# One more PSUM bank for the transposing and gelu tiles, other gather rates, and another DRAM layout of the gate matrix in a one-layer hybrid encoder kernel

## The chip, the cores and the metric

The kernel runs on one core of one Trainium2 chip. The metric is the device time of one execution in microseconds (us). One launch computes the whole layer.

## What is computed

The reference is one layer over 16 learned meta tokens and 1024 tokens of width 1024, in float32:

```
n  = rmsnorm(h)
h += W_out( sig(g_a) * W_oa(MLA(n)) + sig(g_b) * W_ob(GLA(n)) )
h += PEER(rmsnorm(h))
```

MLA is chunk-causal attention with 8 heads, GLA a gated linear attention with 4 heads. PEER is a mixture of 16384 one-row experts: for each token, 8 heads choose 16 experts each, by the two best-16 lists of 128 sub-keys; the output is

```
out[t] = sum over the 128 chosen e of  gate[t,e] * gelu(u[e] . n2[t]) * v[e]
```

The change lies in the PEER part and in the buffers of the mixing part.

## The kernel before, in words

**Stages.** Tokens come in two groups of 512. MLA of group 0, mix and route of group 0, MLA of group 1, mix of group 1 (`mix`, about 1290 to 1680 us), route of group 1 (`route`, about 1690 to 1950 us), then `dense` until the end. Each float32 product is three matmuls (`mm3`) on a high and a low part of each operand: `split` (lines 78 to 82) casts the high part on ScalarE (L79) and subtracts the low part on VectorE (L80).

**Two ways to do the experts.** Tokens 0 to 447 are done by gather (tokens 384 to 447 split differently from the rest): `gather_all` fetches rows of u and v by index, 128 rows of 4 KB each time, with an indirect DMA issued by GpSimd (L115), and VectorE does the dot (L1361) or the add into the output (L1377) for each. There are 832 such steps in all, on 6 row buffers (`NROW`). The generator is drawn forward by `bg`: each call of `weights` (one 512 KB weight tile) draws `self.rate` steps. The rates are the `R_` constants: 2.4 in the building of the gate matrix, 2.5 (`R_VONLY`) while only V stages run, 3.3 (`R_DENSE`) after that. A gather waits for the high cast of the weight tile that came before it in the program (`self.pace`).

**The dense way.** The other 640 tokens (five blocks of 128, `DB`) are multiplied with all experts, 128 groups of 128 experts. `u_stage` makes the gelu of one group (48 matmuls in two halves, each half in one PSUM bank of tag `tr`, read by the gelu on ScalarE, L1466). `v_stage(q, half)` takes four groups (`EG`), scales their activations by the gates (`coef`, L1504 copies the last 64 columns on ScalarE, L1505 multiplies the others on VectorE), splits them, and accumulates in five banks of tag `mm`, which VectorE adds into `acc` (L1530). The u stages of the first 58 groups (`NLEAD`) are done ahead and their activations kept in DRAM (`d_act`). From V stage 25 on, two u stages stand between two V stages.

**The gate matrix.** `gate_matrix` builds gate[expert, token] from one-hot products, 32 tokens at a time, in a stage tile of 16 KB per partition, and stores it to DRAM in `d_gate` (L1628): 20 stores of 2 MB. In the same stretch (1950 to about 2325 us) 31 lead u stages run. In `dense`, `gates(q, k, 4)` loads a quarter of one four-group's gates (L1492): 128 loads of 320 KB.

**Order.** Loads and stores of the program are issued by the SP queue in order. Within each engine the order of instructions is set at build time by a planner that simulates the program with its own costs, earlier lines of the program first; a wait at the head of an engine holds all that stands behind it. Weight tiles are loaded one ahead: raw tile, high and low part have two buffers each.

**PSUM.** There are 8 banks. In the mixing and the dense part, tag `tr` has 2 and tag `mm` 5.

Of the kernel before, what the change touches and what calls it, by code (L numbers as in the profile page):

```python
# [17 lines left out]
PSUM = bass.MemoryType.PSUM  # L18
DRAM = bass.MemoryType.DRAM

P = 128
# [7 lines left out]
NC = D // P  # L29
# [3 lines left out]
NK = 128  # L33
# [7 lines left out]
ND = len(DB) * P  # L41
# [4 lines left out]
EG = 4  # L46
# [11 lines left out]
BANKS = [dict(zip(("S", "tr", "mm", "pv"), map(int, str(x)))) for x in (BA, BB)]  # L58
NGA, NGR, F_MLA = 14, 14, 0.9
RA0, NRU, NLATE = 7, 22, 5  # L60
R_MLA, R_MIX, R_ROUTE, R_BUILD, R_VONLY, R_DENSE = 0.0, 2.8, 0.7, 2.4, 2.5, 3.3


class Layer:
# [94 lines left out]
    def build(self, debug=None):  # L159
# [12 lines left out]
        with ExitStack() as ctx:  # L172
            tc, nc, a = self.tc, self.nc, self.a
# [11 lines left out]
            dt = lambda n, s: dram.tile(s, F32, name=n)  # L185
# [14 lines left out]
            self.d_act = dt("d_act", [NLEAD, P, NU])  # L200
            self.d_n2t = dt("d_n2t", [2, P, NC, NU - GT])
            self.d_wl = dt("d_wl", [NKEPT, P, D])
            self.d_gate = dt("d_gate", [P, ND // 32, NK * 32])
            self.small = self.pool(ctx, "small", 3)
            self.sm = self.small
            with ExitStack() as c0:
# [11 lines left out]
                first = self.pool(early, "ck1", side="right")  # L218
# [299 lines left out]
    def mla_heads(self, ctx):  # L518
# [16 lines left out]
        for u in range(HA * 2):  # L535
# [9 lines left out]
            if gi == 0:  # L545
                self.merge(vals, fill)
                if h + 1 < HA:
                    self.load_wkv(h + 1)
                    self.head_tiles(h + 1)
                if u % 4 == 0 and h + 2 < HA:  # L550
                    if u == 0:
                        self.load_wq(1)
                    self.pair_tiles(h // 2 + 1)
                for f in late_fns:
                    f()
                    self.bg(self.rate)
                    self.beside(F_MLA)
            else:
                mix = []
                for i in range(max(len(fill), len(late_fns))):  # L560
                    mix += fill[i:i + 1] + late_fns[i:i + 1]
                self.merge(vals, mix)
# [238 lines left out]
    def mix_pools(self, ctx):  # L801
        if self.grp == 0:
            self.g1 = self.pool(ctx, "yA")
        self.psum = self.pool(ctx, "gpsum", 2, space=PSUM)
        self.wk = self.pool(ctx, "gw", 2)
        if self.grp == 0:
            self.arp = self.pool(ctx, "arpA", 2)
        if self.grp == 0:
            self.wp = self.wk
        self.nj = "gt"  # L810
        with self.tc.high_priority(offset=400):
            self.ya = self.load_ya(self.grp)
# [131 lines left out]
    def mix(self, g):  # L944
        nc = self.nc
        st = [{} for _ in range(4)]
        if g:
            self.warm(WARM[1], "mm", 5)
        first = self.gla_proj(g, 0, st[0], ("w_oa", 0))
        next(first)  # L950
        self.gla_logs(g)
        self.run(first)
        inner = self.gla_inner(g, 0, st[0])
        self.weave(self.branch_a(g, *self.ya), inner, 0.8)
        self.yb = self.t(self.g1, [P, NC, GT], F32R, "yh"), self.t(self.g1, [P, NC, GT], F32R, "yl")
        first = (NGA, NGR)[g]
        for h in range(1, 4):
            nxt = ("w_gq", h + 1) if h < 3 else (self.gate_keys() + [("w_ob", 0)])[first]
            self.weave(self.gla_proj(g, h, st[h], nxt), inner, 1.8)
            self.run(inner)  # L960
            inner = self.gla_inner(g, h, st[h])
        self.weave(self.raw_gates(g, range(first, 2 * NC), ("w_ob", 0), "tr", 2), inner, 1.0)
        self.run(inner)
        if g == 0 and NGF:
            self.fetch_n(self.nh, self.nl)
        self.run(self.branch_b(g))
# [499 lines left out]
            self.nc.scalar.activation(at[:, ts], ps[:, :HD], AF.Gelu)  # L1466

    def lead_gate(self, key, nxt):
        self.run(self.raw_gate(1, self.gate_keys().index(key), nxt, "tr", 2))

    def lead_u(self, key, nxt):
        e = key[1]
# [6 lines left out]
    def dense(self, ctx):  # L1479

        nc, a = self.nc, self.a
        self.psum = self.pool(ctx, "dpsum", 2, space=PSUM)
        self.wk = self.pool(ctx, "dw", 2)
        ng = NK // EG
        ndb = len(DB)
# [2 lines left out]
        def gates(q, k, n):  # L1488
            if q >= ng:
                return  # L1490
            bs = slice(k * ND // 32 // n, (k + 1) * ND // 32 // n)
            nc.sync.dma_start(gbuf[:, q % 2, bs].rearrange("p b e t -> p b (e t)"), self.d_gate[:, bs, q * EG * 32:(q + 1) * EG * 32])  # L1492

        def load_act(e):
            if e < NLEAD:
# [3 lines left out]
        def coef(q, j):  # L1499
            cf = coefs[q, j] = self.t(self.wk, [P, 2, ND], F32R, "cf", NCF)  # L1500
            at = acts.pop(q * EG + j)
            at3 = at.rearrange("p (b t) -> p b t", t=32)
            m = NU // 32
            nc.scalar.copy(at3[:, m:], gbuf[:, q % 2, m:, j])  # L1504
            nc.vector.tensor_tensor(at3[:, :m], at3[:, :m], gbuf[:, q % 2, :m, j], ALU.mult)  # L1505
            self.split(cf[:, 0], cf[:, 1], at)

        def v_stage(q, half):
            ps = [self.t(self.psum, [P, 512], F32, "mm", 5) for _ in range(ndb)]
            for i in range(EG // 2):  # L1510
                key = ("vb", q * EG // 2 + i, half)
                wh, wl = self.weights(key, order.get(key))
                gates(q + 2, 2 * half + i, 4)
                if q == 0 and half == 0:
                    for k in (2 * i, 2 * i + 1):
                        gates(1, k, 4)
                if q == 0 and i == EG // 2 - 1:
                    cs = slice(half * 512, (half + 1) * 512)
                    for k, b in enumerate(DB):
                        nc.sync.dma_start(acc[:, k, cs], self.d_h[b * P:(b + 1) * P, cs])  # L1520
                for j in range(2):
                    e = 2 * i + j
                    cf = coefs[q, e]
                    s = slice(j * 512, (j + 1) * 512)
                    for b in range(ndb):
                        ts = slice(b * P, (b + 1) * P)
                        self.mm3(ps[b], cf[:, 0, ts], cf[:, 1, ts], wh[:, s], wl[:, s], e == 0, e == EG - 1)
            for b in range(ndb):
                o = acc[:, b, half * 512:(half + 1) * 512]
                nc.vector.tensor_tensor(o, ps[b], o, ALU.add)  # L1530
# [29 lines left out]
        gbuf = self.t(self.wk, [P, 2, ND // 32, EG, 32], F32, "big")  # L1560
        for k in range(4):
            gates(0, k, 4)
# [11 lines left out]
        for x in seq[nlead:]:  # L1574
            if x[0] == "v":
                q, half = x[1:]
# [15 lines left out]
    def gate_matrix(self):  # L1592

        nc = self.nc
        G8 = 8
        iota = self.iota[:, None, :].broadcast_to([P, G8, NK])
        for d, blk in enumerate(DB):
            pk = self.picks[blk]  # L1600
            while blk == HB and not self.half_done:
                next(self.G)
            stage = self.t(self.wk, [P, NK, 32], F32, "big")
            pt = self.t(self.psum, [P, 4, P], F32, "tr")
            for i in range(2):
                nc.tensor.transpose(pt[:, i], pk["ij"][:, i].rearrange("p h k -> p (h k)"), self.ident)
            nc.tensor.transpose(pt[:, 2], pk["gate"].rearrange("p h k -> p (h k)"), self.ident)
            tt = self.t(self.wk, [P, ND], F32, "at", NAT)[:, 0:3 * P].rearrange("p (a t) -> p a t", a=3)
            nc.scalar.copy(tt, pt[:, 0:3])
            yield  # L1610
            for t32 in range(4):
                if t32:
                    stage = self.t(self.wk, [P, NK, 32], F32, "big")
                for q in range(4):
                    oh, gh = [self.t(self.wk, [P, 2 * ND], F32, "cf", NCF)[:, 0:NK * G8].rearrange("p (t j) -> p t j", j=NK) for _ in range(2)]
                    t = t32 * 32 + q * G8
                    tb = lambda i: tt[:, i, t:t + G8, None].broadcast_to([P, G8, NK])
                    for k in range(G8):
                        nc.vector.tensor_scalar(gh[:, k], self.iota, tt[:, 1, t + k:t + k + 1], tt[:, 2, t + k:t + k + 1], ALU.is_equal, ALU.mult)  # L1619
                    nc.vector.tensor_tensor(oh, iota, tb(0), ALU.is_equal)  # L1620
                    for k4 in range(2):
                        ps = self.t(self.psum, [P, 4, NK], F32, "mm", 5)
                        for k in range(4):
                            kk = k4 * 4 + k
                            self.gm_last = nc.tensor.matmul(ps[:, k], oh[:, kk], gh[:, kk], start=True, stop=True)  # L1625
                        nc.scalar.copy(stage[:, :, q * G8 + k4 * 4:q * G8 + k4 * 4 + 4], ps.rearrange("p k j -> p j k"))
                        yield
                nc.sync.dma_start(self.d_gate[:, d * 4 + t32], stage.rearrange("p j t -> p (j t)"))  # L1628


def host(inputs):
# [71 lines left out]
```

## Time and profile before

| | |
|---|---|
| median of 3 runs | 3832.95 us (3827.49 to 3835.6) |
| the profiled execution's own time | 3828.28 us |
| its span, first to last instruction | 3826.5 us |
| TensorE (PE) busy | 3551.3 us, 93% |
| VectorE (DVE) busy | 2999.0 us, 78% |
| ScalarE (ACT) busy | 1320.1 us, 34% |
| GpSimd (POOL) busy | 1523.7 us, 40% |
| mean granted TensorE clock | 0.968 |

PE leads in the whole, but the shares differ from stage to stage: from 1950 us on, DVE is busy for nearly as long as PE. Matmuls are pipelined, so a busy PE is not PE at its peak.

### The profile page before, as it was taken

The page shows a single profiled execution, that of the slowest core. Times are in us where ns is not written, and L with a number is a line of the kernel's source. Part 1 is how long each engine was busy: PE and PEld are TensorE (multiplying, and loading weights), DVE is VectorE, ACT ScalarE, POOL GpSimd, SP SyncE. Part 2 cuts the span into 40 slices and gives each one's busy share as a digit, 9 for nine tenths or more (in the row PEclk, how much of TensorE's full clock was granted, in tenths as well). Part 3 has the DMA queues.
Part 4 walks back from the last instruction along what each step waited for, and adds up shares of the span by engine and source line. Part 5 has one row for each costly group of instructions (what it writes and reads, how often), then busy time and mean ns, then how long its engine had stood idle before and what let it go on. Part 6 is the DMA issues. An engine that isn't in the chain of part 4 may idle for free.

```text
span 3826.5 us, 56688 instructions
## 1 busy us (share of the span) xinstructions
PE 3551.3 (93%) x20380; PEld 3088.1 (81%) x20385; DVE 2999.0 (78%) x6559; ACT 1320.1 (34%) x2851; POOL 1523.7 (40%) x1199
## 2 busy tenths in 40 slices
PE   8899998999799999899999998999999999999996
PEld 8787797777688788679898997777788888888885
DVE  5545444379877667559999997999988988898898
ACT  4656333232366334222244333222222222222221
POOL 2432333334332344322232223444455555555555
PEclk9999999999899999899999999999999999999998
DMA  4544634665324998665567879999999889999888
GB/s 160 173 159 141 222 131 130 192 212 186 124 69 114 341 353 299 268 225 203 171 227 275 288 280 372 332 342 344 332 334 338 303 315 325 322 348 322 298 324 318
DMA packets 390779, 976.98 MB, mean 255 GB/s; under 512 B 40464, under 2 KB 155664, under 8 KB 387680
## 3 DMA queue, kind: packets, MB, share of 16 engines
q1 hardware_dynamic: 242048, 508.50, 37.8%
q0 software_dynamic: 148448, 464.86, 34.6%
q8 instruction: 160, 2.62, 0.3%
q14 instruction: 123, 1.01, 0.1%
HBM read 825.61 MB, written 147.51 MB: 254 GB/s over the span
## 4 chain that ended last, share of the span: by engine, by line
PE 31%; DVE 24%; DMA 9%; issue 5%; ACT 1%; SPq 0%; POOL 0%; ACTq 0%; DVEq 0%; POOLq 0%
PE mm L86 6%; PE mm L87 6%; PE mm L88 6%; DVE cf L1619 4%; DVE acc L1377 3%; DVE row L1361 3%; DVE wl L80 3%; PE tr L88 3%; PE tr L86 3%; DMA wr<-in_uT 3%; PE tr L87 3%; DVE cf L1620 2%; DVE big L1530 2%; DMA row<-in_u,ids 2%; DMA row<-in_v,ids 1%
## 5 line engine op out<-in xcount | busy, mean ns | idle before, releaser
L115 POOL DMA_INDIRECT row<-in_v,ids x384 | 494.6, 1288 | 692.3 <-DVE acc L1377 274.1
L115 POOL DMA_INDIRECT row<-in_u,ids x384 | 479.5, 1249 | 590.8 <-issue 129.9
L86 PE MATMUL tr<-ar,wh 128*128 128x288 f32 x2048 | 616.9, 302 | 32.0 <-ACT at L1466 32.0
L79 ACT CAST wh<-wr 128x1024 fp32r<-128x1024 f32 x344 | 360.4, 1048 | 747.9 <-PE mm L88 302.8
L87 PE MATMUL tr<-ar,wh 128*128 128x288 f32 x2048 | 610.8, 299 | 0.0
L88 PE MATMUL tr<-ar,wl 128*128 128x288 f32 x2048 | 602.7, 301 | 8.5 <-DVE wl L80 8.1
L1361 DVE CUSTOM_DVE_ANT_0 row<-row,n2b 128x1024 f32<-128x1024 f32 x448 | 544.1, 1221 | 60.8 <-DMA row<-in_u,ids 51.0
L87 PE MATMUL mm<-wl,cf 128*128 128x512 f32 x1280 | 508.9, 398 | 5.1 <-DVE wl L80 5.0
L1377 DVE SCALAR_TENSOR_TENSOR acc<-row,act,acc 128x1024 f32<-128x1024 f32 x384 | 491.9, 1281 | 22.2 <-DMA row<-in_v,ids 20.0
L88 PE MATMUL mm<-wh,cf 128*128 128x512 f32 x1280 | 507.8, 397 | 0.0
L86 PE MATMUL mm<-wh,cf 128*128 128x512 f32 x1280 | 443.8, 398 | 15.0 <-DVE big L1530 8.6
L86 PEld LDWEIGHTS tr<-ar,wh 128*128 128x128 f32 x2048 | 392.4, 192 | 38.8 <-ACT at L1466 36.6
L80 DVE TENSOR_TENSOR wl<-wr,wh 128x1024 fp32r<-128x1024 f32 x264 | 324.6, 1229 | 103.2 <-ACT wh L79 98.9
L88 PEld LDWEIGHTS tr<-ar,wl 128*128 128x128 f32 x2048 | 387.5, 191 | 11.7 <-DVE wl L80 11.7
L87 PEld LDWEIGHTS tr<-ar,wh 128*128 128x128 f32 x2048 | 392.3, 192 | 2.1
L80 POOL TENSOR_TENSOR wl<-wr,wh 128x1024 fp32r<-128x1024 f32 x80 | 194.4, 2433 | 326.2 <-ACT wh L79 307.2
L86 PEld LDWEIGHTS mm<-wh,cf 128*128 128x128 f32 x1280 | 238.1, 188 | 80.5 <-ACT wh L79 9.9
L87 PEld LDWEIGHTS mm<-wl,cf 128*128 128x128 f32 x1280 | 241.9, 189 | 65.7 <-DVE wl L80 8.2
L88 PEld LDWEIGHTS mm<-wh,cf 128*128 128x128 f32 x1280 | 242.0, 189 | 58.8
L1530 DVE TENSOR_TENSOR big<-mm,big 128x512 f32<-128x512 f32 x320 | 204.4, 680 | 19.0 <-PE mm L88 18.9
L1466 ACT ACTIVATE at<-tr 128x288 f32<-128x288 f32 x212 | 87.0, 410 | 345.9 <-PE tr L88 326.1
L1625 PE MATMUL mm<-cf,cf 128*128 128x128 f32 x1280 | 158.4, 277 | 28.5 <-DVE cf L1620 28.5
(448 smaller groups left out, 7747.6 us busy)
## 6 DMA issues: line engine op xcount, KB each, us to landing
wr<-in_uT SPq DMA_DIRECT2D x128, 512.0 KB
wr<-in_vb SPq DMA_DIRECT2D x128, 512.0 KB
d_gate<-big SPq DMA_DIRECT2D x20, 2048.0 KB
big<-d_gate SPq DMA_DIRECT2D x128, 320.0 KB
d_wl<-wl SPq DMA_DIRECT2D x72, 512.0 KB
wl<-d_wl SPq DMA_DIRECT2D x72, 512.0 KB
at<-d_act SPq DMA_DIRECT2D x58, 288.0 KB
wr<-in_w_q SPq DMA_DIRECT2D x32, 512.0 KB
```

What stands on the lines that cost most here:

```text
L79: self.pace = self.nc.scalar.copy(hi, src)
L80: i = (eng or self.nc.vector).tensor_tensor(lo, src, hi.bitcast(F32), ALU.subtract)
L86: first = mm(ps, lh, rh, start=start, stop=False)
L87: mm(ps, lh, rl, start=False, stop=False)
L88: self.pe_last = mm(ps, ll, rh, start=False, stop=stop)
L115: i = self.nc.gpsimd.indirect_dma_start(out=out, out_offset=None, in_=self.a[table], in_offset=bass.IndirectOffsetOnAxis(ap=idx, axis=0))
L1361: lag(nc.vector.tensor_tensor_reduce(out=u, in0=u, in1=held[b][0], op0=ALU.mult, op1=ALU.add, scale=1.0, scalar=0.0, accum_out=act[:, 0, k ...
L1377: lag(nc.vector.scalar_tensor_tensor(acc, v, act[:, 1, k:k + 1], acc, ALU.mult, ALU.add))
L1466: self.nc.scalar.activation(at[:, ts], ps[:, :HD], AF.Gelu)
L1530: nc.vector.tensor_tensor(o, ps[b], o, ALU.add)
L1619: nc.vector.tensor_scalar(gh[:, k], self.iota, tt[:, 1, t + k:t + k + 1], tt[:, 2, t + k:t + k + 1], ALU.is_equal, ALU.mult)
L1625: self.gm_last = nc.tensor.matmul(ps[:, k], oh[:, kk], gh[:, kk], start=True, stop=True)
```

## The change

- The pools `gpsum` and `dpsum` get 3 buffers as the default in place of 2, so tag `tr` has three banks (with `mm`'s five, all eight); two calls that named 2 for `tr` name 3.
- `R_VONLY` goes from 2.5 to 2.6, `R_DENSE` from 3.3 to 3.5.
- `d_gate` lies as [partition, four-group, token block, 4 x 32] in place of [partition, token block, 128 x 32]. A quarter load is then one run of 2560 B per partition in place of 5 runs of 512 B; a store is 32 runs of 512 B per partition in place of one of 16 KB.
- For the first four-group (q = 0), the copy of the last 64 gate columns is made by VectorE in place of ScalarE.

```
-R_MLA, R_MIX, R_ROUTE, R_BUILD, R_VONLY, R_DENSE = 0.0, 2.8, 0.7, 2.4, 2.5, 3.3
+R_MLA, R_MIX, R_ROUTE, R_BUILD, R_VONLY, R_DENSE = 0.0, 2.8, 0.7, 2.4, 2.6, 3.5
...
-            self.d_gate = dt("d_gate", [P, ND // 32, NK * 32])
+            self.d_gate = dt("d_gate", [P, NK // EG, ND // 32, EG * 32])
...
-        self.psum = self.pool(ctx, "gpsum", 2, space=PSUM)
+        self.psum = self.pool(ctx, "gpsum", 3, space=PSUM)
...
-        self.weave(self.raw_gates(g, range(first, 2 * NC), ("w_ob", 0), "tr", 2), inner, 1.0)
+        self.weave(self.raw_gates(g, range(first, 2 * NC), ("w_ob", 0), "tr", 3), inner, 1.0)
...
-        self.run(self.raw_gate(1, self.gate_keys().index(key), nxt, "tr", 2))
+        self.run(self.raw_gate(1, self.gate_keys().index(key), nxt, "tr", 3))
...
-        self.psum = self.pool(ctx, "dpsum", 2, space=PSUM)
+        self.psum = self.pool(ctx, "dpsum", 3, space=PSUM)
...
-            nc.sync.dma_start(gbuf[:, q % 2, bs].rearrange("p b e t -> p b (e t)"), self.d_gate[:, bs, q * EG * 32:(q + 1) * EG * 32])
+            nc.sync.dma_start(gbuf[:, q % 2, bs].rearrange("p b e t -> p (b e t)"), self.d_gate[:, q, bs].rearrange("p b x -> p (b x)"))
...
-            nc.scalar.copy(at3[:, m:], gbuf[:, q % 2, m:, j])
+            (nc.scalar.copy if q else nc.vector.tensor_copy)(at3[:, m:], gbuf[:, q % 2, m:, j])
...
-                nc.sync.dma_start(self.d_gate[:, d * 4 + t32], stage.rearrange("p j t -> p (j t)"))
+                nc.sync.dma_start(self.d_gate[:, :, d * 4 + t32], stage.rearrange("p (q e) t -> p q (e t)", e=EG))
```

## Rows read from the trace of the kernel before

**Rows 1.** Busy time by stage: window, length, PE, PEld, DVE, ACT, POOL, PEclk, DMA, GB/s.
```profile
1950.00:2300.00 350.00, 324.01 (x2574) 318.39 (x2574) 349.97 (x809) 137.29 (x241) 77.27 (x68) 1.00 0.77 276
2340.00:2370.00 30.00, 19.22 (x123) 18.99 (x123) 15.79 (x19) 7.87 (x17) 9.12 (x7) 0.77 1.04 408
2420.00:2760.00 340.00, 329.69 (x1392) 259.22 (x1390) 325.10 (x431) 88.07 (x140) 149.53 (x118) 1.00 0.95 339
...
3260.00:3500.00 240.00, 238.05 (x1381) 212.85 (x1380) 219.72 (x282) 65.82 (x111) 137.96 (x106) 1.00 0.93 333
3500.00:3660.00 160.00, 150.54 (x822) 133.77 (x822) 129.76 (x164) 36.92 (x65) 84.28 (x65) 0.95 0.87 304
...
2760.00:3794.00 1034.00, 1003.14 (x5655) 888.85 (x5653) 914.57 (x1168) 261.87 (x440) 582.29 (x449) 0.99 0.91 322
```

**Rows 2.** Waits of ScalarE, 2760 to 3793: total us, times, longest us.
```profile
ACT wh L79 <- DMA wr<-in_uT: 99.8, 9, 14.5
```

**Rows 3.** Timeline of one late weight load: start, us, engine, line, [idle before <- releaser].
```profile
3505.30 4.13 SPq L1492 DMA_DIRECT2D big<-d_gate  x3
3509.53 1.19 SPq L908 DMA_DIRECT2D wr<-in_uT  x1
...
3524.13 1.04 ACT L79 CAST wh<-wr 128x1024 fp32r<-128x1024 f32 x1 [13.52 <-DMA wr<-in_uT]
...
3525.20 1.23 DVE L80 TENSOR_TENSOR wl<-wr,wh 128x1024 fp32r<-128x1024 f32 x1 [6.36 <-ACT wh L79]
...
3525.54 0.61 PE L86 MATMUL tr<-ar,wh 128*128 128x288 f32 x1 [2.64 <-ACT at L1466]
...
3527.89 1.68 POOL L115 DMA_INDIRECT row<-in_v,ids  x1 [9.99 <-DVE acc L1377]
```

**Rows 4.** The page's line of DMA packets.
```profile
DMA packets 390779, 976.98 MB, mean 255 GB/s; under 512 B 40464, under 2 KB 155664, under 8 KB 387680
```

**Rows 5.** Timeline of SP and ScalarE between gate building and the first V stage.
```profile
2337.58 1.08 SPq L1492 DMA_DIRECT2D big<-d_gate  x2
2338.70 9.74 SPq L1520 DMA_DIRECT2D big<-d_h  x1
2348.55 1.19 SPq L1551 DMA_DIRECT2D d_act<-at  x1
...
2355.47 0.68 ACT L1504 COPY at<-big 128x64 f32<-128x64 f32 x4 [7.38 <-DMA big<-d_gate]
...
2361.10 0.41 ACT L1466 ACTIVATE at<-tr 128x288 f32<-128x288 f32 x1 [3.40 <-DMA d_act<-at]
```

**Rows 6.** Waits of TensorE over the whole span: total us, times, longest us.
```profile
PE tr L86 <- ACT at L1466: 32.0, 20, 10.8
```

**Rows 7.** Windows, as Rows 1: stores in 512 B pieces, then a 2 MB gate store.
```profile
87.50:90.00 2.50, 2.50 (x17) 2.50 (x16) 0.00 (x0) 0.00 (x0) 0.00 (x0) 1.00 0.94 284
...
2065.00:2070.00 5.00, 3.97 (x34) 3.81 (x34) 5.00 (x7) 2.35 (x4) 0.61 (x1) 1.00 1.05 419
```

**Rows 8.** Timeline of one gate store and the weight tile behind it.
```profile
2309.55 0.32 SPq L1628 DMA_DIRECT2D d_gate<-big  x1
2313.02 0.33 SPq L908 DMA_DIRECT2D wr<-in_uT  x1
...
2319.79 1.05 ACT L79 CAST wh<-wr 128x1024 fp32r<-128x1024 f32 x1 [2.39 <-PE tr L87]
...
2322.96 1.21 DVE L80 TENSOR_TENSOR wl<-wr,wh 128x1024 fp32r<-128x1024 f32 x1
```

**Rows 9.** Gathers (L115) alone in a window: length, POOL busy (x), PEclk, DMA, GB/s.
```profile
2760.00:3794.00 1034.00, 582.29 (x449) 0.99 0.91 322
```

**Rows 10.** The end: adds of gathered rows (ns min/median/max), then output stores on SP.
```profile
L1377 DVE SCALAR_TENSOR_TENSOR acc<-row,act,acc x17: 1269/1285/1285, 3794.5 to 3820.9; 128x1024 f32<-128x1024 f32 x17
...
3791.06 6.09 SPq L1588 DMA_DIRECT2D out<-big  x5
3822.19 0.33 SPq L1379 DMA_DIRECT2D out<-acc  x1
```

## The prediction

> **What bounds the kernel now.** I read the page first (PE 93% of the span, DVE 78%), then the busy time by stage, then in each stage who was waited for, and last the timeline around the longest waits. Four stages matter [rows 1].
>
> While the gate matrix is built (1950 to 2300) DVE is busy 349.97 of 350 us, PE 324: DVE sets the time there. Between building and V stages (2340 to 2370) PE works only 19.2 of 30 us, at a mean clock of 0.77. In the V-only stretch (2420 to 2760) PE has 329.7 and DVE 325.1 of 340 us. In the mixed stretch (2760 to 3794) PE is busy 1003.1 of 1034 us. So PE bounds it, but unevenly: 3260 to 3500 loses 2 us of 240, while 3500 to 3660 loses 9.5 us and runs at 0.95. After 3794 PE has nothing left; 17 adds of gathered rows run until 3822 and the last output store until 3826.5 [rows 10].
>
> The uneven losses have one look. ACT waits 99.8 us in nine times for a weight tile from DRAM [rows 2]. In one of them [rows 3] SP issues three gate loads (its queue is held for 4.13 us), the uT tile goes out behind them at 3509.53, and its cast starts only at 3524.13, after 13.5 idle us of ACT. Everything in order behind that cast waits: the low part on DVE, PE for 2.64 us, the next gather for 9.99 us because no row buffer is freed. PE's clock falls after it; the stretch 3500 to 3660 holds three of the nine.
>
> **The change part by part.** The sum is made on the profiled execution: 3828.28 us, span 3826.5 us. The median of the runs is 4.7 us above it, which I add at the end.
>
> *Gate loads in pieces of 2560 B.* Of the packets in the trace, 155,664 are under 2 KB [rows 4]; the 128 gate loads are 128 x 640 = 81,920 pieces of 512 B, so these pieces must be packets of their own. The change makes 16,384 of them, with the same bytes. What a gate load costs the queue is seen between the stages: two loads (0.66 MB) issued at 2337.58 have landed at 2355.47, 17.9 us later, while the DMA engines moved 408 GB/s, 7.3 MB in all [rows 1, 5]; most of that was gathers, whose rows come in 4 KB pieces. So a load in 512 B pieces gets a small part of the engines as long as gathers are in flight, and the uT tile behind it in SP's queue waits for it. Price in the mixed stretch: the losses of PE are 30.9 us of idle time plus about 10 us of clock (0.99 of 1034) [rows 1]. All of it is the upper bound (41 us); nothing is the lower, if the late tiles are late by bytes and not by pieces, since gates and gathers together fill the engines (share 0.91) in any case. I take 18, a little under half, because the share stays near full and more gathers come in.
>
> The Trainium skill ("DMA: Bandwidth & Descriptors", Queues, rings and completion order) says that each DMA engine takes turns between its queues, one whole packet a turn. The trace agrees with it [rows 3, 5]; by it a 512 B piece against a 4 KB gather piece would get one part in nine, and a 2560 B piece five in thirteen.
>
> *Between building and V stages.* There SP stood 9.74 us on its next load behind the two gate loads, so the store of an activation went out only at 2348.55 and the gelu that needs its buffer waited until 2361.10; ACT before that waited 7.38 us for the gates [rows 5]. PE's one wait of 10.8 us is this [rows 6]. With 256 pieces in place of 1280, both waits shorten. Bounds: 0 and 17.7 us (10.8 idle, up to 6.9 of clock over 30 us [rows 1]). I take 10: the last gate store, which these loads need, lands later (below).
>
> *Copy of q = 0 on DVE.* Four copies of 64 columns, under 0.25 us each by their time on ACT [rows 5]. ACT's next work is the cast of the same coefficients, which needs the same gates, so it is held all the same. 0.
>
> *Third bank.* PE waited 32.0 us for gelus in 20 times [rows 6], 10.8 of it priced above. In the others the gelu stands behind the late cast: in the one shown [rows 3] the cast ends at 3525.17 and PE starts at 3525.54, and its third matmul needs the low part that ends at 3526.43. So a free bank gains at most 0.37 us of 2.64; 19 times that is 7 us. But the planner may order the engines anew from the mix stage on, which no row prices; I bound it by the largest single stall the trace shows, 11 us either way. Value: 4 us gained.
>
> *Pace.* 50 V-only calls at 0.1 more bring 5 steps earlier, five calls after building one more. DVE had 15 us free there and a step costs it 1.28 us [rows 1, 10]: 6.4 us, hidden; PE has 10 us free as well, and with that cover gone it would cost the 6.4. In the mixed stretch 148 calls asked for 488 steps at 3.3, and 449 were issued [rows 9]: the buffers, not the asking, held them. So 3.5 alone issues no more; what frees gathers is the end of the blocked time (nine events of up to 10 us, at one gather in 2.3 us up to 39 gathers). Against it stands DVE: 914.6 busy of 1034 us, 88%; with 17 more steps in a stretch 18 us shorter it is 936 of 1016, 92%.
>
> *The end.* Without the adds behind PE, the five output stores (2.6 MB, issued from 3791.06, 6.4 us at 408 GB/s) would end near 3803 [rows 1, 10]. So the end is worth 0 to 23 us. Six steps come earlier by count and some more by the freed time; I take 12.
>
> *Gate stores in pieces of 512 B.* Each of the 20 stores is 4096 pieces. A 2 MB store ran at 419 GB/s (5.0 us); 512 B stores with no gather beside them ran at 284 GB/s [rows 7], which makes 7.4 us, and SP is held meanwhile. The uT tile often goes out right behind (3.5 us later here; 12 of 20 within 4 us) [rows 8]. Its cast ended at 2320.84 and DVE reached the low part at 2322.96, so 2.1 us of slip cost nothing. With 2.4 us from the pieces and about 1 from a gather that takes its turns first, 1.3 us shows on DVE, twelve times: 16 us. Lower bound 0 (where the cast is earlier than this, as DVE's lack of idle time suggests), upper bound below, with the slower rival. I take 8.
>
> The skill's same page (Specifications) puts line rate at 512 B and up; by that the stores would lose nothing and the sum would be 8 us better. The row of 284 GB/s says otherwise, and the row decides.
>
> **Sum.** 18 + 10 + 4 + 12 - 8 = 36 us gained: 3828.3 - 36 = 3792 profiled, 3797 as a median.
>
> **The rivals.**
> *All of it comes (3744 to 3775).* Late tiles vanish, the clock stays up, gathers end before PE: 41 + 17.7 + 7 + 23 = 89 us at most, 3744. For it: the undisturbed 240 us [rows 1]. Against: DVE would be at 95% and DMA above 0.95.
> *Bytes, not pieces (3817).* The gate loads and gathers in flight are the same bytes, the tiles stay late, and only the bank, the pace and a part of the end remain: 4 + 12 = 16 us. For it: share 0.91 with windows over 1.0. Against: 17.9 us for 0.66 MB.
> *The waits only move (no change, 3833).* A larger part for SP's loads makes gathers land later, DVE waits for rows in place of tiles, the end grows by what PE gains.
> *The stores starve the building stage (slower, 3853).* Now the stores are the small pieces and lose their turns. Two or three gathers in flight take 524 KB each, 1.25 us at 419 GB/s: 2.4 + 3.75 = 6.1 us of slip a store at most, 4.0 us past the cover, 80 us over 20 stores, all on DVE, which has none to give. It decides from a slip of 4.3 us a store, where 20 x 2.2 = 44 us eat the other gains (18 + 10 + 4 + 12). At 5.3 us it costs 64, net 20: 3853. For it: no idle on DVE. Against: only 68 gathers in 350 us [rows 1], so mostly one is in flight at a time.
>
> **How the numbers follow.** A difference of 0.2% (7.7 us) is about what a measurement of this kernel can tell from none. Forecast 3797 (3776 to 3812): 0.48. All of it: 0.17. Bytes: 0.14, nearly all of it still faster by 0.2%. Waits move: 0.10. Slower: 0.11. Faster 0.77, same 0.12, slower 0.11. The range 3758 to 3836 leaves out the far part of the first rival and most of the last.
>
> **What would show it.** Right: the waits of ACT for uT under 40 us, the three-load SP entries near 1 us, the gate loads between the stages landed in under 9 us, at most 8 adds after PE's last matmul. Wrong, if: the building stage has idle time on DVE before low parts and grows by over 15 us; SP stands for more than 5 us on gate stores; the tiles stay late although the gate loads land early; or adds after PE's end stay at 17 although the tiles come in time.

## The result, and the profile after

The changed kernel took 3794.66 us in the median of 6 runs (3791.53 to 3801.6), the kernel before, on the same chip, 3829.69 us (6 runs, 3824.69 to 3835.6): a ratio of 0.9929, 95% interval 0.9914 to 0.9944. The forecast was 3797. The profiled execution took 3791.53 us, its span is 3789.8 us.

Busy time by stage, after, in the windows and columns of [rows 1]:
```profile
1950.00:2300.00 350.00, 329.07 (x2582) 327.13 (x2581) 344.79 (x794) 134.47 (x241) 91.57 (x68) 0.97 0.84 273
2340.00:2370.00 30.00, 22.59 (x164) 21.65 (x162) 16.80 (x25) 7.51 (x15) 11.21 (x9) 0.97 1.02 391
2420.00:2760.00 340.00, 321.45 (x1341) 251.83 (x1340) 318.15 (x422) 85.25 (x136) 148.76 (x117) 0.99 0.92 334
3260.00:3500.00 240.00, 240.00 (x1402) 215.57 (x1401) 218.00 (x277) 64.93 (x110) 133.13 (x106) 1.00 0.92 331
3500.00:3660.00 160.00, 160.00 (x935) 143.76 (x934) 147.69 (x189) 43.54 (x74) 94.75 (x73) 1.00 0.93 340
2760.00:3794.00 1034.00, 998.65 (x5712) 889.43 (x5710) 943.50 (x1193) 265.77 (x444) 590.54 (x459) 0.99 0.91 333
```
Two rows stand out. From 3500 to 3660, where PE had lost 9.5 us and clock, it now works all 160 us at 1.00. In the V-only window PE does less than before, 321.45 against 329.69 us: there the change lost. (The last row reaches past PE's end at 3767, so it holds 27 us in which PE has nothing to do.)

The same place in the program as [rows 3], after; start, us, engine, line, [idle before <- releaser]:
```profile
3491.72 1.28 SPq L1492 DMA_DIRECT2D big<-d_gate  x3
3493.09 0.68 SPq L908 DMA_DIRECT2D wr<-in_uT  x1
...
3505.39 1.05 ACT L79 CAST wh<-wr 128x1024 fp32r<-128x1024 f32 x1 [8.88 <-DMA wr<-in_uT]
...
3506.47 1.22 DVE L80 TENSOR_TENSOR wl<-wr,wh 128x1024 fp32r<-128x1024 f32 x1 [1.53 <-ACT wh L79]
...
3509.16 1.68 POOL L115 DMA_INDIRECT row<-in_v,ids  x1 [5.17 <-DVE acc L1377]
```
SP's three gate loads hold its queue for 1.28 us, not 4.13, and the tile behind them arrives 12.3 us after its issue, not 14.6. ACT still waits 8.88 us. But DVE now idles 1.53 us, not 6.36, and PE does not wait at all. At this place the path has a cover, a wait of ACT that costs PE nothing, of between 8.9 and 13.5 us; only what goes past it costs. From the first gate load's issue to the cast it is 13.7 us, not 18.8; of the 5.2 us gained 2.9 are the shorter hold of SP's queue and the rest the faster landing.

The trace also records every DMA packet, and these show how a tile is held up. Before, from 3514 to 3523, SP's queue got 931 packets through (804 gate pieces of 512 B, 127 of the tile in 4 KB) beside 669 gather packets of 4 KB: 0.93 MB against 2.74. After, from 3498 to 3507, it got 527 (305 of 2560 B, 222 of 4 KB) beside 506: 1.69 MB against 2.07. So next to gathers the queue's share goes roughly by packets and not by bytes. That small pieces keep the DMA engines busy for longer adds little: a packet of 512 B took 27 ns and one of 2560 B 102 ns, so five small ones take 135, which over three gate loads and 16 engines makes 0.8 us.

Waits of ACT and of PE in the mixed stretch, after (total us, times, longest us):
```profile
ACT wh L79 <- DMA wr<-in_uT: 58.1, 9, 8.9
```
```profile
PE mm L86 <- DVE big L1530: 4.0, 2, 3.8
PE mm L86 <- ACT wh L79: 0.9, 1, 0.9
```
There are nine late tiles as before [rows 2] (twelve in e15, a second profile of this kernel), none over 8.9 us, and the wait of PE for gelus [rows 6] is gone from this stretch.

The page's packet line, after:
```profile
DMA packets 404602, 976.97 MB, mean 258 GB/s; under 512 B 40464, under 2 KB 155664, under 8 KB 404064
```
The number under 2 KB is the same as in [rows 4], to the packet: the 81,920 pieces of 512 B of the loads are gone and the 20 x 4096 of the stores have come. The change moved small pieces from the loads to the stores.

Between building and V stages, after, as [rows 5]:
```profile
2340.33 0.79 SPq L1492 DMA_DIRECT2D big<-d_gate  x2
...
2342.51 10.06 SPq L1520 DMA_DIRECT2D big<-d_h  x8
...
2346.91 0.20 DVE L1504 COPY at<-big 128x64 f32<-128x64 f32 x1 [4.88 <-DMA big<-d_gate]
...
2368.62 0.76 DVE L1505 TENSOR_TENSOR at<-at,big 128x576 f32<-128x576 f32 x1 [7.70 <-DMA at<-d_act]
2369.41 0.72 ACT L79 CAST cf<-at 128x640 fp32r<-128x640 f32 x1 [4.41 <-DVE at L1505]
```
and PE's longest wait there (2330 to 2384):
```profile
PE mm L86 <- ACT wh L79: 7.1, 1, 7.1
```
The gates are used at 2346.91, 6.6 us after their issue (17.9 before). SP still stands 10.06 us on the residual rows (9.74 and 11.57 before). PE's wait of 10.8 us for a gelu is gone, but another of 7.1 us has come: DVE waits 7.70 us for a stored activation to come from DRAM, and in ACT's order the first V stage's weight cast stands behind the coefficients made from it.

The end, after, as [rows 10]:
```profile
L1377 DVE SCALAR_TENSOR_TENSOR acc<-row,act,acc x12: 1275/1285/1286, 3767.2 to 3784.4; 128x1024 f32<-128x1024 f32 x12
...
3762.53 5.11 SPq L1588 DMA_DIRECT2D out<-big  x5
3785.75 0.33 SPq L1379 DMA_DIRECT2D out<-acc  x1
```

**The stages of all profiles.** Each from one profiled execution, in us: last key score of the second route (L1285), from there to the last gate store, to the first add of a V stage (L1530), the V-only stretch to the first gelu after it, the mixed stretch to the last add of a V stage, the end to the last add of a gathered row. They are differences of starts and ends in the traces.

| kernel | to last key score | building | transition | V-only | mixed | end |
|---|---|---|---|---|---|---|
| before | 1899.1 | 426.8 | 56.3 | 384.7 | 1027.0 | 27.0 |
| after | 1886.9 | 443.0 | 54.4 | 396.9 | 985.4 | 17.8 |
| after, again (e15) | 1900.7 | 444.1 | 53.0 | 393.6 | 986.2 | 17.3 |
| layout alone (e14) | 1900.3 | 426.6 | 55.0 | 383.0 | 993.3 | 26.1 |
| the same (e2) | 1899.5 | 444.9 | 59.4 | 384.0 | 993.3 | 27.1 |
| bank alone (e1) | 1896.2 | 439.9 | 53.4 | 391.8 | 1018.5 | 27.1 |
| all but the layout (e6) | 1890.4 | 440.9 | 54.0 | 398.0 | 1013.5 | 17.6 |
| after, padded (e5) | 1900.1 | 447.9 | 57.0 | 397.2 | 1020.2 | 17.9 |
| after, 2 banks (e7) | 1903.3 | 426.7 | 58.5 | 380.8 | 985.8 | 19.7 |
| after, old pace (e8) | 1890.3 | 446.3 | 53.9 | 385.2 | 985.4 | 27.0 |
| after, pace 2.4 and 3.9 (e10) | 1892.4 | 444.3 | 56.0 | 383.3 | 987.4 | 28.1 |
| after, loads in pairs (e11) | 1890.7 | 441.1 | 53.8 | 394.7 | 986.3 | 17.7 |
| third bank in group 0 alone (e12) | 1891.6 | 443.7 | 58.0 | 377.0 | 986.3 | 19.8 |
| after, copy on ACT (e13) | 1886.6 | 444.4 | 52.5 | 394.4 | 986.2 | 17.7 |

Two profiles of one kernel agree within 4.4 us in the last four columns; the first differs by up to 14, and building once by 18.

### The profile page after: what moved, and what is told of

It is laid out like the page before. It is cut to its first block, busy times and chain, and to the rows that moved or that the text cites. A ratio compares the mean times of both kernels' runs of the same rounds, so it can differ in the third digit from the quotient of the medians.

```text
span 3789.8 us, 56702 instructions
## 1 busy us (share of the span) xinstructions
PE 3532.6 (93%) x20385; PEld 3083.2 (81%) x20385; DVE 2995.9 (79%) x6563; ACT 1318.3 (35%) x2849; POOL 1538.9 (41%) x1199
## 4 chain that ended last, share of the span: by engine, by line
PE 45%; DVE 15%; DMA 6%; issue 3%; ACT 1%; POOL 0%; SPq 0%; DVEq 0%; ACTq 0%; POOLq 0%
PE mm L86 8%; PE mm L87 8%; PE mm L88 8%; PE tr L88 5%; PE tr L86 5%; PE tr L87 5%; DVE cf L1619 3%; DVE row L1361 2%; DVE acc L1377 2%; DVE wl L80 1%; DVE cf L1620 1%; PE mm L1625 1%; DVE big L1530 1%; DMA wr<-in_uT 1%; DMA at<-d_act 1%
## 5 line engine op out<-in xcount | busy, mean ns | idle before, releaser
L115 POOL DMA_INDIRECT row<-in_v,ids x384 | 498.2, 1297 | 698.1 <-DVE acc L1377 253.6
L115 POOL DMA_INDIRECT row<-in_u,ids x384 | 489.1, 1274 | 527.0 <-ACT wh L79 158.0
L86 PE MATMUL tr<-ar,wh 128*128 128x288 f32 x2048 | 608.2, 298 | 17.9 <-ACT wh L79 16.2
L79 ACT CAST wh<-wr 128x1024 fp32r<-128x1024 f32 x344 | 360.4, 1048 | 758.6 <-PE mm L88 340.1
L87 PE MATMUL tr<-ar,wh 128*128 128x288 f32 x2048 | 604.4, 296 | 0.0
L88 PE MATMUL tr<-ar,wl 128*128 128x288 f32 x2048 | 593.3, 298 | 6.6 <-DVE wl L80 6.5
L86 PEld LDWEIGHTS tr<-ar,wh 128*128 128x128 f32 x2048 | 386.9, 189 | 21.7 <-ACT wh L79 17.3
L87 PEld LDWEIGHTS tr<-ar,wh 128*128 128x128 f32 x2048 | 386.7, 189 | 1.9
L1530 DVE TENSOR_TENSOR big<-mm,big 128x512 f32<-128x512 f32 x320 | 204.5, 679 | 23.0 <-PE mm L88 22.9
L1466 ACT ACTIVATE at<-tr 128x288 f32<-128x288 f32 x212 | 86.9, 411 | 337.2 <-PE tr L88 330.6
L79 ACT CAST cf<-at 128x640 fp32r<-128x640 f32 x128 | 93.1, 728 | 279.2 <-PE mm L88 265.0
```

Of the source, the lines that this page charges most:

```text
L79: self.pace = self.nc.scalar.copy(hi, src)
L86: first = mm(ps, lh, rh, start=start, stop=False)
L87: mm(ps, lh, rl, start=False, stop=False)
L88: self.pe_last = mm(ps, ll, rh, start=False, stop=stop)
L115: i = self.nc.gpsimd.indirect_dma_start(out=out, out_offset=None, in_=self.a[table], in_offset=bass.IndirectOffsetOnAxis(ap=idx, axis=0))
```

## The experiments

Ratios are to the kernel before, run beside each on the same chip, with 95% intervals. All of them lie within 1.1% of it.

**Pieces or bytes: two controls.** Both keep the order of the instructions on every engine of the changed kernel. In e5_pad the loads are in 512 B pieces again:
```
-            self.d_gate = dt("d_gate", [P, NK // EG, ND // 32, EG * 32])
+            self.d_gate = dt("d_gate", [P, NK // EG, ND // 32, EG * 40])
... (loads and stores take [..., :EG * 32] of it)
```


> The changed kernel, but each token block's 512 B of the gate matrix is followed by 128 unused bytes in DRAM, so that a gate load is 5 runs of 512 B per partition again, with the same bytes; the stores stay runs of 512 B, and the order on every engine is that of the changed kernel. Theory (the size of the load's pieces makes the weight tiles late): the late uT tiles come back, ScalarE waits 90 us or more for uT between 2760 us and the end of the dense stretch, and the time is 3815 to 3840. Rival (the gain is the new order and the bank, pieces do nothing): 3790 to 3800.

e6_nolayout has the old layout of `d_gate`, loads and stores, and the rest of the change.

> The changed kernel with the gate matrix laid out as before (loads in 512 B pieces, stores in 16 KB pieces); same order on every engine. Theory of the pieces: 3815 to 3835, late uT tiles as in the run with padding; the difference to that run is the price of the small stores, which were put at 8 us. Rival (the order and the bank): 3790 to 3800. Second rival (small stores cost much, small loads nothing): under 3788.

Measured: e5_pad 3842.31 us, 1.0029 (1.0015 to 1.0043), 2 us above the theory's range; e6_nolayout 3830.52 us, 0.9996 (0.998 to 1.0011), inside it. Waits of ACT and of PE in the mixed stretch of e5_pad:
```profile
ACT wh L79 <- DMA wr<-in_uT: 104.0, 10, 14.6
```
```profile
PE tr L86 <- ACT wh L79: 15.8, 9, 3.7
PE tr L88 <- DVE wl L80: 4.2, 9, 0.8
```
The same bytes in the same order, cut in five, bring the late tiles back, and PE waits nine times for their casts. With the old layout (e6_nolayout), where the pieces lie elsewhere in DRAM, ACT waits 121.3 us in 14 times, the longest 13.5. So it is the pieces. The rival in which the tiles are late by bytes falls, and so does any account by bank or pace alone. With three banks the waits stand under the cast's name (L79) that stood under the gelu's (L1466) before: the gelus had been late because of the cast, as the prediction read it. The duration of a gate load on SP's queue (min/median/max ns) in the kernel before, after, and e5_pad says the same:
```profile
L1492 SPq DMA_DIRECT2D big<-d_gate x128: 370/520/7137, 2316.3 to 3635.2; - x128
```
```profile
L1492 SPq DMA_DIRECT2D big<-d_gate x128: 319/427/1662, 2318.8 to 3602.1; - x128
```
```profile
L1492 SPq DMA_DIRECT2D big<-d_gate x128: 370/532/6491, 2338.8 to 3657.1; - x128
```
Padding makes the stride 640 B, and e5_pad is 11.8 us slower than e6_nolayout, 7 of it in building and 7 in the mixed stretch, where no gate is stored. So not all of it can be the small stores; what the stride costs by itself is not separated.

**One part alone.** e2_layout is the kernel before with the layout, e1_bank with the third bank in all four places.

> The kernel before with the new layout alone; the order on every engine is that of the kernel before. Theory of the pieces: 3795 to 3812, the stretch of V and u stages 20 to 40 us shorter, the building stage 0 to 8 us longer, the adds after TensorE's last matmul still about 17. Rival (bytes, the order makes the gain): 3822 to 3838.

> The kernel before with the third bank alone. In the changed kernel the first 1270 us were 14 us shorter, and only the bank touches them. Theory (the bank gives that, by a new order in the mix stage of group 0): 3812 to 3822. Rival (as forecast, 4 us): 3822 to 3830. Second rival (later stages give it back, since the building stage was longer in the changed kernel): 3828 to 3840.

Measured: e2_layout 3810.89 us, 0.9948 (0.9929 to 0.9967), the theory's range, but with a building stage 18 us longer than before where 0 to 8 were expected (its second run, e14, has none of it); e1_bank 3827.46 us, 0.9985 (0.9969 to 1.0001), the first rival's range and not clear of no change. PE's waits in the mixed stretch of the layout alone (e14):
```profile
PE mm L86 <- ACT wh L79: 3.4, 5, 0.7
PE tr L86 <- ACT at L1466: 2.9, 12, 0.2
PE tr L88 <- DVE wl L80: 2.8, 2, 2.3
```
With two banks the wait for gelus is 2.9 us, against 21.2 us in 19 times before ([rows 6] less its longest). The layout alone took it away.

**What the rest adds.** e7_nobank is the changed kernel with 2 banks in the four places, e8_nopace with the old `R_VONLY, R_DENSE = 2.5, 3.3`, e10_dense39 with 2.4 and 3.9. e11_whole joins the gate loads in pairs:
```
-                gates(q + 2, 2 * half + i, 4)
+                gates(q + 2, half, 2) if i == 0 else None
```


> The changed kernel with two banks again; layout, pace and copy as changed. The third bank alone gave 0.9985. If it is worth the same here, the time is 0.9929 + 0.0015 = 0.9944 of before (3810). Rival: once the gate loads come in time it is the bank that lets PE go on while a gelu is late; then the waits of PE for gelus come back in the mixed stretch (before: 21.2 us in 19 there; changed kernel: under 1) and the time is 0.996 or more. Second rival: the bank only moves work between stages, 0.993, with the mix stage of the first group some 10 us longer and the rest as much shorter.

Measured: 3790.61 us, 0.9919 (0.9891 to 0.9947). The second rival: the way to the log gates of the second group is longer (1255.1 us against 1241.1 and 1251.1 in the two profiles of the changed kernel), building and V-only are 16 us shorter each. PE's wait for gelus in the mixed stretch is 2.6 us.

> The changed kernel with the pace of before (2.5 and 3.3); layout, bank and copy as changed. Theory: the pace is what shortened the end (27.0 to 17.8 us from the last add of the V stages to the last add of all) and what lengthened the V-only stretch (384.7 to 396.9 us); with it undone the end is near 27 us, the V-only stretch near 385 and the mixed one near 994, and as these nearly cancel the time is 0.993 to 0.996 of before (3803 to 3818). Rival (the prediction's step: the end gets shorter by what the late tiles held back, not by the pace): the end stays near 18 us and the time at 0.993. Second rival: the pace costs more in the V-only stretch than it brings, and the time is 0.990.

Measured: 3792.23 us, 0.9916 (0.9892 to 0.9939). End 27.0 and V-only 385.2 us are the theory's, the mixed stretch (985.4) is not, and with it the time is below the theory's. The shorter end is the pace's work and not that of the vanished waits; it is paid for in the V-only stretch.

> The changed kernel with pace 2.4 in the V-only stretch and 3.9 in the mixed one (2.6 and 3.5 in the changed kernel). If the row buffers limit the gathers in the mixed stretch, asking for more there brings none: the V-only stretch is some 12 us shorter, the end 9 or more us longer (near 30), and the time is 0.992 to 0.995. Rival: now that the loads come in time, the asking limits the gathers; then 3.9 brings them, the end shrinks below 17 us though the V-only stretch is shorter as well, and the time is 0.988 to 0.991, faster than the changed kernel.

Measured: 3796.58 us, 0.9926 (0.9903 to 0.995), the theory. Gathers in the mixed stretch (POOL busy, count) of the changed kernel, then of this one:
```profile
2781.00:3767.00 986.00, 571.29 (x443) 1.00 0.92 336
```
```profile
2776.00:3763.00 987.00, 582.39 (x443) 1.00 0.93 335
```
443, and 445 in 1027 us in the kernel before: the order is written at build time, so neither a higher rate nor the time saved by earlier tiles brings one gather more.

> The changed kernel with its gate loads in the dense stage joined in pairs: half as many, each with pieces of 5120 B in place of 2560. If the size of a piece against a gather's 4 KB piece still sets how late a uT tile comes, the waits of ACT for uT fall from 58 us to under 40 and the time to 0.990. Rival: 2560 B is enough and what is left is bytes: the waits stay near 58 us in nine and the time at 0.993. Second rival: a tile behind twice the bytes in SP's queue is later: waits over 80 us, time 0.996.

Measured: 3793.27 us, 0.9927 (0.9903 to 0.9952). The time is the first rival's, the waits are not: they fall to 41.1 us in seven, longest 8.5. Those that went were under cover.

**The changed kernel again, two variants, the layout.** These four ran beside each other. e12_bank0 keeps the third bank in the first group's mix stage only:
```
-        self.psum = self.pool(ctx, "gpsum", 3, space=PSUM)
+        self.psum = self.pool(ctx, "gpsum", 2 if self.grp else 3, space=PSUM)
... ("tr", 2 if g else 3 in mix; dpsum 2)
```


> The changed kernel with its third bank in the mix stage of the first token group alone; two banks in that of the second group, in building and in the dense stage. In the profiles, kernels with the third bank reached the log gates of the second group 8 to 14 us earlier and then took 13 to 20 us longer from the last key score to the last gate store (443 and 446 us against 427). Theory: the gain is made in the first group and the loss by the planner's other order in the second; then the first stays near 1244, the building stage near 427, the V-only stretch near 381, and the time is 10 to 14 us below that of the changed kernel (0.989 to 0.990 of before). Rival: what is early is only waited for later, since DVE bounds the building stage and has the same work to do: building 440 or more and 0.992 as before.

Measured: 3779.69 us (5 runs, 3777.97 to 3789.4), 0.9894 (0.9876 to 0.9913), beside 3798.17 us for the changed kernel: 18.5 us faster by the medians (14 by the means), and the lowest median here. But not as the theory had it: building stays at 443.7 us, and the gain is the V-only stretch, 377.0 us. Waits of PE there (2420 to 2760), in the changed kernel and in e12_bank0:
```profile
PE mm L86 <- DVE big L1530: 15.0, 16, 3.1
```
```profile
PE mm L86 <- DVE big L1530: 4.1, 6, 2.2
```
In the changed kernel PE waits for the adds that free the accumulators (tag `mm`); with two banks in the dense part it mostly does not. It takes the pace as well: three banks with the old pace (e8) wait 7.4 us. Why the planner's order for both together makes these adds late was not looked into.

> The changed kernel with all copies of 64 columns on ACT, as before the change; PE's order is the same, DVE's differs in 20 lines. Theory (the prediction): the copy on DVE is worth 0, and the time is that of the changed kernel within 0.1%. Rival: the first gelus of the V-only stretch come earlier with it, up to the 5.9 us in which the transition of layout alone was longer (59.4 against 53.9 us with copy, layout and bank): 0.15% slower than the changed kernel.

Measured: 3795.73 us, 0.9936 (0.9918 to 0.9954), 2.4 us under the changed kernel's median: the copy is worth nothing that shows.

> The layout alone, a second time (0.9948 the first time), beside the changed kernel. With copy and pace it was 0.9919, with copy and bank 0.9916. Theory: the layout is all of the change, what the others add is under 0.1%, and this run gives 0.993 or less. Rival: bank or pace, either of them, adds some 8 us: 0.995 again.

Measured: 3801.63 us, 0.9954 (0.9936 to 0.9972). The theory falls, narrowly: by the mixed stretch bank and pace together add some 8 us to the layout, and either of them does (e7, e8), but the interval overlaps that of the changed kernel below, and the medians of the two differ by 3.5 us.

> The changed kernel itself, to stand beside the three others on the same chip. All theories: 0.992 to 0.994.

Measured: 3798.17 us, 0.9928 (0.991 to 0.9947).

## Why the prediction was right, step by step

The total came within 2.4 us, but by terms that erred in both directions and cancelled: against the sum, the mixed stretch gave 23.6 us more, the transition 8.1 and the end 2.8 less, and the V-only stretch lost 12.2 that stood at nothing. The mechanism of the first term was right; that the sum came out so close is luck. In the profiles, before less after:

- *Late tiles in the mixed stretch: taken 18, measured 41.6* (1027.0 less 985.4 us), the upper bound. PE did the same work (5617 matmuls against 5614) in 978.6 busy us, not 996.1, and idled 7.4, not 31. This is the term that was mis-sized. The layout alone gives 33.7 of it in both its profiles; bank or pace the other 8. (Taken out of the changed kernel, in e6, it gives 28.1.) I had halved the bound because bytes and share stayed near full; the error was to take "tiles still late" for "PE still loses". Nine tiles are still late, and the sign "under 40 us of ACT's waits" was the wrong sign: 58.1 us cost PE nothing, since none exceeds the cover. The cover differs from place to place: a wait of 10.7 us in e8 cost PE 0.4, one of 9.9 us in the kernel before 3.8. The Trainium skill ("DMA: Bandwidth & Descriptors", Queues, rings and completion order) has one packet a turn for each queue. The packets counted above, 931 beside 669 and 527 beside 506, agree roughly, with each piece a packet of its own; e5_pad agrees too, but SP's longer hold comes with the small pieces as well, and no run parts the two.
- *Transition: taken 10, measured 1.9.* The gates came early, as said (used 6.6 us after issue, limit 9). What is late next was missed: PE's wait of 10.8 us for a gelu went, and one of 7.1 us behind a stored activation's load came in its place.
- *Copy: taken 0, measured 0* (e13).
- *Third bank: taken 4, alone 0.9985, some 6 us, not clear of nothing.* The bound of 11 either way held in total, but the planner's reordering moved more than that between stages: in ten profiles with the bank in group 0 the second group's log gates (L1030) came at 1241 to 1251 us, in four without at 1252 to 1255; building and the V-only stretch gave it back. With the copy, the pace and the layout in place, the bank adds nothing (e7).
- *Pace: taken 0 by itself, and 12 at the end.* The end got 9.2 us shorter, and by the pace: five adds fewer, 12 left, not the 8 of the sign. The other part, gathers brought by the freed time, did not come: 443 in place of 445. And the five steps were not hidden in the V-only stretch: it grew by 12.2 us, a term that I had priced at up to 6.4 and left out. Most of the loss comes from bank and pace together: with the layout, 2.6 with two banks gives 380.8 us and three banks with 2.5 give 385.2 (the bank alone, with the old layout, 391.8).
- *Stores: taken 8 lost, measured about 0.* From the first to the last gate store it is 353.5 us in the kernel before, 353.3 in the layout alone (e14) and 353.4 in e7; in the order of the changed kernel 358.8 and 359.8, against 358.2 with the old stores (e6). One profile stands out, 370.0 in e2, the program of e14 again (below). The lower bound was right, and the packets show why: from issue to its last packet a store took 7.6 us in the mean before, 9.4 in e14 and 9.8 in e7. The slip is 1.8 to 2.2 us, not the 3.4 of the prediction, and so within the 2.1 us of cover that it had read, or nearly. The Trainium skill's same page (Specifications) puts line rate at 512 B and up, by which nothing would be lost. The time agrees, the rate does not: a packet of 512 B took 27 ns and one of 16 KB 611, 19 against 27 bytes in a ns.

The rivals: "bytes, not pieces" falls with e5_pad, "the waits only move" with the mixed stretch, and the slower one (starving stores) with the stores' slip, which decided only from 4.3 us on. "All of it comes" was right for the mixed stretch alone.

Left open: why the orders made by bank or pace each take 8 us off the mixed stretch once the layout is there (PE idles 6 to 8 us in place of 10.7 and works 978 to 980 in place of 983, at the same matmuls); why building is 440 us or more with the third bank; and how much of the 18.5 us of e12_bank0 is its early bank, since e7, with none, was not run beside it. Of building, this much can be read: from the last key score to the first gate store it is 83 to 84 us in every kernel with the third bank there and 73 to 75 in those with two, so some 10 of the 16 us lie ahead of the first store; e12, with two, loses its 16 us between the stores instead. The layout's 33.7 us in two profiles stand against 18 to 21 us in the medians: e14's profile was of its fastest execution (3791.75 us), and e2's holds the 18 us in building.

## What to carry to other kernels

Make long pieces where a transfer shares a queue with tiles that someone waits for, and let the short ones fall where nothing close behind is needed: the same 81,920 pieces cost about 20 us or more as loads and about nothing as stores. Do not price a wait by its total on an engine off the path; look for how long it may be before the bounding engine waits, and count only what goes past. And set a buffer count by stage: a bank or a pace that helps in one stage changes a build-time order in all the later ones.

## What the hardware showed beside

SP's queue was held up to 7.1 us by a single gate load of 640 pieces in the kernel before (10.4 in e1), and at most 1.7 us by one of 128 in the changed one (2.2 in e12). Two executions of one program (e2 and e14) differ by 18 us in building alone; in the longer one the gather issues on GpSimd took 2.97 and 2.54 us in the mean and one 14.2 us. First e2, then e14, the gathers of v:
```profile
L115 POOL DMA_INDIRECT row<-in_v,ids x33 | 98.0, 2970 | 87.5 <-DVE acc L1377 51.1 <-ACT wh L79 20.5 <-ACT big L1626 9.8
```
```profile
L115 POOL DMA_INDIRECT row<-in_v,ids x36 | 39.6, 1100 | 121.3 <-DVE acc L1377 81.2 <-ACT big L1626 26.5 <-ACT wh L79 8.7
```
(columns: busy us and mean ns, then the idle time before). The cause was not found. The small stores need not be it: e6, with the old ones, has an issue of 12.7 us. It warns against reading a stage's difference under some 20 us in building from one profile each.
